# Opening of a two-layer transformer block: how c's rows reach the partitions, and which channels VectorE and TensorE sum

## Chip, cores and metric

The kernel runs on one core of a Trainium2 chip. The metric is device time in microseconds (us): the median of several executions. The kernel before takes 1632.78 us, the median of 3 runs (1631.76 to 1633.01).

## What is computed

The reference is a two-layer diffusion transformer with 256 latent tokens `x` and 256 context tokens `ctx`, 1024 features each. Each layer has a half feed-forward block, a mixer (attention, then mLSTM), and another half feed-forward block. Only the opening matters here: the modulation of the tokens by `c` (for latent tokens) and `c_ctx` (for context tokens), and the first product with the first feed-forward weights.

```
mod_lat = split(silu(c) @ ada_w[0] + ada_b[0], 9)       # 9 channels of 1024 numbers
mod_ctx = split(silu(c_ctx) @ ada_w[0] + ada_b[0], 9)
xm = h * (1.0 + scale) + shift                          # channels 0 (shift) and 1 (scale)
a, u = split(xm @ w_in, 2)
y = (silu(a) * u) @ w_out
```

So before the first token can be multiplied, two channels of `silu(c) @ ada_w` are wanted, for both vectors: 2 channels x 1024 features x 2 vectors, each a sum over 1024 numbers.

## The kernel before

**Tiles.** Features lie on the 128 partitions, in ND = 8 blocks `d` of 128; the 512 tokens (256 latent, then 256 context) lie along the free axis. Every f32 product is made of three F32R products: high part by high part, high by low, low by high. A value is split by a rounding copy on ScalarE (the high part) and a subtraction on VectorE (the low part).

**The opening, `start` (L1440 to L1599).** It loops over the eight feature blocks `d`. For each, a block of tokens (`in_xt`, 256 KB), a block of weights for the first four hidden tiles (`in_start_in`, 448 KB) and the block's two channels of `ada_w` (512 KB each) are loaded, all on SP's queue, in the order in which the code issues them. A channel is summed in one of two ways, by the table `PEDOT` (L48), which lists for each `d` the channels that go to TensorE:

- on TensorE (`by_pe`, L1488): 8 weight tiles of 128x128 from `in_ada_p`, each multiplied with two columns of silu(c) (`b.ct`), so 8 matmuls of 128x2 into the PSUM tile `dots`; ScalarE adds the bias (`moved`, L1498). Block 0 does both its channels in another form (`first_by_pe`, L1479: 8 matmuls of 2x256, a copy on ScalarE at L1483, two matmuls that turn the rows into columns, and a bias on VectorE at L1502);
- on VectorE (`by_dve`, L1504): for each vector one `scalar_tensor_tensor` of 128x1024 (L1510), which multiplies a row block of `ada_w` (`in_ada_w`) with `b.cb` and sums along the free axis. `b.cb` holds silu(c) and silu(c_ctx) repeated on all 128 partitions, 2 x 1024 numbers. A channel is two such dots; the bias follows at L1502.

`b.cb` is filled by two DMAs of 512 KB each (`silu_load`, L298 to L300: one row read 128 times), and ScalarE applies Silu to it in place (`silu`, L310).

When block `d`'s four numbers per feature are there, `modulated` (L1513) makes the modulated tokens by four ScalarE activations at L1525 (two of high parts, two in full), and `low` (L1530) subtracts to give the low parts: two 128x256 subtractions of tokens, one 128x896 subtraction of weights, on VectorE. ScalarE casts the weights at L1477, and also scales the raw tokens for later (L552). Then `products(d, i)` (L1546) gives 7 matmuls of 128x512 for each of i = 0 (high by high), 1 (high weights by low tokens) and 2 (low weights by high tokens), into seven PSUM tiles. The eighth output tile is made by `fill`, 3 matmuls per block, placed ahead of blocks 6 and 7 and at the end (`FILLED`, `EIGHTH`). After the opening the ordinary feed-forward units follow: their matmuls stand at L241, their casts at L225 and subtractions at L230, the gate at L579 and L580.

**What sets the order.** Nearly every instruction of `start` is pinned to program order on its engine (`pin`), so each engine runs them in the order of the code, each waiting for its own inputs. In the loop over `d` at L1565 that order is: load tokens and weights of block d+2, and channels of block d+3; cast the weights of block d+1; TensorE's dots for block d+1 (d of 2 and more); products(d, 0); low parts of block d's tokens; products(d, 1); for d below 2 TensorE's and VectorE's dots for block d+1; ScalarE's bias and the four activations for block d+1; low parts of the weights of d+1; for d of 1 and more VectorE's dots for block d+2; products(d, 2). DMAs use eight semaphores in turn, so an issue waits until the DMA eight places ahead of it has landed. Small work tiles `tmp` come from six buffers.

Of the kernel before, what the change touches and what calls it, by code (L numbers as in the profile page):

```python
# [11 lines left out]
BF16 = mybir.dt.bfloat16  # L12
# [9 lines left out]
T = 512  # L22
# [22 lines left out]

NSTART = 4

PEDOT = {0: (0, 1), 1: (1,), 2: (1,), 4: (1,), 6: (1,)}  # L48

WARM = 5  # L50

# [121 lines left out]
class Body:  # L173
# [23 lines left out]
    def mm(self):  # L197
        return self.t([P, 512], tag="mm", bufs=6, pool=self.pp)
# [218 lines left out]
    def pin(self, ins):  # L417

        return self.tc.keep_in_program_order(ins)
# [1020 lines left out]
def start(b):  # L1440
# [4 lines left out]
    nc, pin = b.nc, b.pin  # L1445
    V, S = nc.vector, nc.scalar
# [5 lines left out]
    ec = b.cols[:, BLOCK:].rearrange("p (d c v) -> p d c v", d=ND, c=2)  # L1452
    raws, blocks, ws, xs = {}, {}, {}, {}

    def load_dots(d):
        if d < ND:
            raws[d] = b.pair(F32)
            chs = PEDOT.get(d, ())
            for ch in range(2):
                if ch not in chs:  # L1460
                    dma(raws[d][ch], b.a["ada_w"][0, ch * ND + d])

            blocks[d] = []
            for i, ch in enumerate(chs):
                r, n = raws[d][ch], len(chs) * P
                dma(r, b.a["ada_p"][list(PEDOT).index(d), i])
                blocks[d] += [r[:, k * n : (k + 1) * n] for k in range(ND // len(chs))]

    def load(d):
        if d < ND:  # L1470
            dma(b.h[:, d, :], b.a["xt"][:, d, :])
            r = b.t([P, 1024], tag="raw", bufs=RAW)[:, : 7 * P]
            dma(r, b.a["start_in"][d][:, : 7 * P])
            ws[d] = [r] + b.pair(n=7 * P)

    def cast(d):
        pin(S.copy(ws[d][1], ws[d][0]))  # L1477
# [10 lines left out]
    def by_pe(d):  # L1488
        for i, ch in enumerate(PEDOT.get(d, ())):
            for k in range(ND):  # L1490
                mm(summed(d)[:, ch, :], blocks[d][k][:, i * P : (i + 1) * P], b.ct[:, k, :], start=k == 0, stop=k == ND - 1)

    def summed(d):
        return dots[:, TL + 4 * d : TL + 4 * d + 4].rearrange("p (c v) -> p c v", c=2)

    def moved(d):
        for ch in PEDOT.get(d, ()):
            pin(S.activation(ec[:, d, ch, :], summed(d)[:, ch, :], AF.Identity, bias=b.b01[:, d, ch : ch + 1]))  # L1498

    def biased(d, chs, x):  # L1500
        n = chs.stop - chs.start
        pin(V.tensor_tensor(out=ec[:, d, chs], in0=x[:, chs], in1=b.b01[:, d, chs, None].broadcast_to([P, n, 2]), op=ALU.add))  # L1502

    def by_dve(d):  # L1504
        chs = [ch for ch in range(2) if d < ND and ch not in PEDOT.get(d, ())]
        if chs:
            z = b.tmp().bitcast(BF16)
            for ch in chs:
                for v in range(2):
                    pin(V.scalar_tensor_tensor(z, raws[d][ch], 1.0, b.cb[:, v, :], ALU.mult, ALU.mult, accum_out=ec[:, d, ch, v : v + 1]))  # L1510
            biased(d, slice(chs[0], chs[-1] + 1), ec[:, d])

    def modulated(d):  # L1513
        jobs = []
# [14 lines left out]
    def low(l, x, h):  # L1529
        return pin(V.tensor_tensor(out=l, in0=x, in1=h.bitcast(F32), op=ALU.subtract))  # L1530
# [15 lines left out]
    def products(d, i):  # L1546
        w, x = ((1, 0), (1, 1), (2, 0))[i]
        for n, o in enumerate(acc):
            mm(o, ws[d][w][:, n * P : (n + 1) * P], b.x(d, BOTH)[x], start=not d and not i, stop=d == ND - 1 and i == 2)

    load_dots(0)
    load(0)
    b.silu_load(pin)
    load_dots(1)
    load(1)
    load_dots(2)
    b.setup_last()
    for _ in range(WARM):
        mm(dots[:, :TL], b.ones, b.ones[:, None, :].broadcast_to([P, 2, P]), start=True, stop=True)
    first_by_pe()  # L1560
    cast(0)
    modulated(0)
    low(ws[0][2], ws[0][0], ws[0][1])
    b.silu(pin)
    for d in range(ND):  # L1565
        n = d + 1
        load(d + 2)
        load_dots(d + 3)
        if d == EIGHTH[0]:
            load_eighth()  # L1570
        if n < ND:
            cast(n)
        if d == EIGHTH[1]:
            pin(S.copy(eighth[1], eighth[0]))
        if d > 1:
            by_pe(n)
        for k in FILLED.get(d, ()):
            fill(k)
        products(d, 0)
        for x in xs[d]:  # L1580
            last = low(*x)
        products(d, 1)
        if d < 2:
            by_pe(n)
            by_dve(n)
        moved(n)
        if n < ND:
            modulated(n)
            low(ws[n][2], ws[n][0], ws[n][1])
        if d:  # L1590
            by_dve(d + 2)
        if d == EIGHTH[1]:
            low(eighth[2], eighth[0], eighth[1])
        products(d, 2)
    fill(ND - 2)
    fill(ND - 1)
    b.fence[last.ins.engine] = last
# [63 lines left out]
def _layout(inputs):  # L1661
# [6 lines left out]
    part = lambda d, chs: w[:, :, list(chs), d].reshape(len(chs), -1, P, len(chs) * P).transpose(0, 2, 1, 3).reshape(-1, P, 1024)  # L1668
    A["ada_p"] = np.stack([np.resize(part(d, chs), (2, P, 1024)) for d, chs in PEDOT.items()])
    A["ada_w"] = f("ada_w").transpose(0, 2, 1).reshape(2, 72, P, D)  # L1670
# [78 lines left out]
```

## Time and profile before

| | us |
|---|---|
| median of 3 runs | 1632.78 (1631.76 to 1633.01) |
| the profiled execution, as timed | 1630.64 |
| its span in the profile | 1628.9 |
| start of the first product of tokens and weights | 10.63 |
| start of the first feed-forward unit after the opening (L241) | 66.01 |
| mean granted TensorE clock of the span | 0.998 |

The profiled execution took 1.74 us outside its span, and 2.14 us less than the median. In the profile, times run from the start of the span. A row of the timeline gives the start, the length, the engine, the line, the operation, the number of merged instructions, and in brackets the idle time before it with what ended it. SPq is the queue of SyncE, which issues the DMAs; PE is TensorE, DVE is VectorE, ACT is ScalarE.

### The profile page before, as it was taken

To read this page: it belongs to the slowest core of one execution; us is meant where nothing else is said; L and a number is where in the kernel's file an instruction comes from. 1 tells how busy PE (TensorE), PEld (TensorE's weight loads), DVE (VectorE), ACT (ScalarE), POOL (GpSimd) and SP (SyncE) were. 2 spreads that over 40 slices of the span, in tenths; PEclk is the share of its full clock that TensorE was granted. 3 is DMA by queue.
4 is the path that set the end of the run, shared out by engine and by line. 5 is a ranking of instruction groups with operands and counts; after the bars stand their busy time and mean duration, and the time that the engine had idled before them with its cause. 6 is when DMAs were issued, how large, how long until landed. Compare 5 with 4: busy or idle time off the path is not lost. (4 is left out here: it accounts for less than half of the span.)

```text
span 1628.9 us, 26573 instructions
## 1 busy us (share of the span) xinstructions
PE 1605.6 (99%) x10298; PEld 1449.8 (89%) x10298; DVE 1353.4 (83%) x2694; ACT 750.3 (46%) x1272; POOL 62.1 (4%) x76
## 2 busy tenths in 40 slices
PE   8999999999999999999999999999999999999998
PEld 6888888889988998889998998889999989999987
DVE  6799977749889879899986879789966968897687
ACT  5532223215676453316652444336652657566542
POOL 0000000001011100000000100000001000020000
PEclk9999999999999999999999999999999999999999
DMA  9677756422202447633345258713363342437552
GB/s 371 219 238 243 243 192 193 141 78 85 65 1 78 144 137 221 216 124 104 123 148 183 78 163 289 250 60 117 104 226 98 98 130 90 140 108 254 181 174 91
DMA packets 72494, 252.58 MB, mean 155 GB/s; under 512 B 7984, under 2 KB 10800, under 8 KB 72368
## 3 DMA queue, kind: packets, MB, share of 16 engines
q1 hardware_dynamic: 71792, 250.10, 47.3%
q8 instruction: 80, 1.31, 0.3%
q10 hardware_dynamic: 576, 0.79, 0.1%
q14 instruction: 46, 0.38, 0.1%
HBM read 249.81 MB, written 1.05 MB: 154 GB/s over the span
## 5 line engine op out<-in xcount | busy, mean ns | idle before, releaser
L241 PE MATMUL t<-t,t 128*128 128x256 f32 (+2 forms) x8412 | 1315.5, 317 | 7.3 <-ACT t L225 3.4
L241 PEld LDWEIGHTS t<-t,t 128*128 128x128 f32 x8412 | 1184.2, 188 | 126.4 <-ACT t L225 4.8
L225 ACT CAST t<-t 128x1024 fp32r<-128x1024 f32 (+3 forms) x521 | 428.5, 844 | 484.7 <-PE t L241 221.9
L230 DVE TENSOR_TENSOR t<-t,t 128x256 fp32r<-128x256 f32 (+2 forms) x740 | 514.0, 729 | 112.6 <-ACT t L225 108.9
L341 DVE SCALAR_TENSOR_TENSOR t<-t,t 128x1024 bf16<-128x1024 f32 x224 | 260.7, 1220 | 0.0
L579 ACT ACTIVATE t<-t 128x512 f32<-128x512 f32 (+1 forms) x71 | 34.3, 489 | 105.5 <-PE t L241 105.5
L932 PE MATMUL t<-t,t 128*128 128x256 f32 (+1 forms) x256 | 79.4, 310 | 0.0
L709 DVE SCALAR_TENSOR_TENSOR t<-t,t,t 128x256 f32<-128x256 f32 x96 | 42.7, 479 | 43.9 <-PE t L241 43.7
L933 PE MATMUL t<-t,t 128*128 128x256 f32 (+1 forms) x256 | 78.6, 307 | 0.1
L934 PE MATMUL t<-t,t 128*128 128x256 f32 (+1 forms) x256 | 78.5, 307 | 0.0
L580 DVE TENSOR_TENSOR t<-t,t 128x512 f32<-128x512 f32 (+1 forms) x71 | 38.9, 553 | 43.5 <-PE t L241 31.3
L475 POOL TENSOR_TENSOR t<-t,t 128x256 f32<-128x256 f32 x30 | 23.4, 780 | 1108.6 <-ACT t L465 1107.2
L1447 PE MATMUL t<-t,t 128*128 128x512 f32 (+2 forms) x276 | 57.3, 363 | 3.8 <-DVE t L1530 2.4
L860 PE MATMUL t<-t,t 128*128 128x512 f32 (+1 forms) x300 | 60.7, 364 | 0.0
L860 PEld LDWEIGHTS t<-t,t 128*128 128x128 f32 x300 | 51.4, 189 | 9.2 <-DVE t L854 0.4
L1447 PEld LDWEIGHTS t<-t,t 128*128 128x128 f32 (+1 forms) x276 | 45.8, 187 | 15.3 <-DVE t L1530 2.9
L465 ACT ACTIVATE t<-t 128x256 f32<-128x256 f32 x72 | 26.2, 413 | 65.7 <-DVE t L458 65.7
L933 PEld LDWEIGHTS t<-t,t 128*128 128x128 f32 x256 | 48.1, 188 | 3.3 <-DVE t L230 0.8
L932 PEld LDWEIGHTS t<-t,t 128*128 128x128 f32 x256 | 48.3, 189 | 2.7
L934 PEld LDWEIGHTS t<-t,t 128*128 128x128 f32 x256 | 48.1, 188 | 2.5
L532 ACT ACTIVATE t<-t,t 128x256 fp32r<-128x256 f32 x72 | 32.8, 503 | 30.1 <-DVE t L531 30.1
L632 DVE TENSOR_TENSOR t<-t,t 128x512 f32<-128x512 f32 x66 | 45.4, 687 | 0.4
(202 smaller groups left out, 1071.7 us busy)
## 6 DMA issues: line engine op xcount, KB each, us to landing
t<-in_ffn_in SPq DMA_DIRECT2D x168, 512.0 KB, 4.0
t<-in_ada_w SPq DMA_DIRECT2D x138, 512.0 KB, 4.2
t<-in_ffn_out SPq DMA_DIRECT2D x66, 512.0 KB, 4.5
t<-in_ffn_last SPq DMA_DIRECT2D x22, 512.0 KB, 3.6
t<-in_att_in SPq DMA_DIRECT2D x12, 512.0 KB, 3.6
t<-in_c SPq DMA_DIRECT2D x8, 512.0 KB, 7.6
t<-in_att_out SPq DMA_DIRECT2D x8, 512.0 KB, 3.6
t<-in_ml_qk SPq DMA_DIRECT2D x8, 512.0 KB, 3.7
```

The source lines that it names most:

```text
L225: self.behind(self.nc.scalar.copy(h, x))
L230: self.behind(self.nc.vector.tensor_tensor(out=ls, in0=xs, in1=hs.bitcast(F32), op=ALU.subtract))
L241: mm = lambda *k, **kw: self.nc.tensor.matmul(*k, skip_group_check=not group, **kw)
L341: ins = nc.vector.scalar_tensor_tensor(self.tmp().bitcast(BF16), r, 1.0, self.cb[:, v, :], ALU.mult, ALU.mult, accum_out=to)
L580: V.tensor_tensor(out=sl, in0=sl, in1=pu[:, :n], op=ALU.mult)
L632: add = lambda o, x, y: V.tensor_tensor(out=o, in0=x, in1=y, op=ALU.add)
L709: V.scalar_tensor_tensor(z, y[:, gg[0] - t0 : gg[1] - t0], gate()[:, v, d : d + 1], z, ALU.mult, ALU.add)
L860: pin(nc.tensor.matmul(o, gs[g], ws[k][w][:, i : i + n], start=k == k0 and g == w == 0, stop=k == k1 - 1 and g == 1,))
L932: mm(o, self.xh[:, k, c], wh, start=k == 0, stop=False)
L933: mm(o, self.xh[:, k, c], wl, start=False, stop=False)
L934: mm(o, self.xl[:, k, c], wh, start=False, stop=k == ND - 1)
L1447: mm = lambda *k, **kw: pin(nc.tensor.matmul(*k, **kw))
```

## The change

The core of the diff:

```diff
-PEDOT = {0: (0, 1), 1: (1,), 2: (1,), 4: (1,), 6: (1,)}
+PEDOT = {0: (0, 1), 1: (1,), 2: (1,), 3: (1,), 4: (1,)}
...
-    def by_dve(d):
+    def by_dve(d, *parts):
         chs = [ch for ch in range(2) if d < ND and ch not in PEDOT.get(d, ())]
-        if chs:
-            z = b.tmp().bitcast(BF16)
-            for ch in chs:
+        for i in parts:
+            if i < len(chs):
+                z, ch = b.tmp().bitcast(BF16), chs[i]
                 for v in range(2):
                     pin(V.scalar_tensor_tensor(z, raws[d][ch], 1.0, b.cb[:, v, :], ALU.mult, ALU.mult, accum_out=ec[:, d, ch, v : v + 1]))
-            biased(d, slice(chs[0], chs[-1] + 1), ec[:, d])
+                if i == len(chs) - 1:
+                    biased(d, slice(chs[0], chs[-1] + 1), ec[:, d])
...
+    rows = [(v, slice(i, i + T), b.tmp()) for v in range(2) for i in (0, T)]
+    for v, c, r in rows:
+        pin((V, nc.gpsimd)[v].memset(r, 0.0))
+    for v, c, r in rows:
+        pin(S.dma_start(r[::32, :], b.a["c2"][v : v + 1, c].broadcast_to([4, T])))
     load_dots(0)
     load(0)
-    b.silu_load(pin)
     load_dots(1)
...
     b.setup_last()
+    for v, c, r in rows:
+        pin(V.stream_shuffle(b.cb[:, v, c], r, [0] * 32))
+    b.silu(pin)
     for _ in range(WARM):
...
     low(ws[0][2], ws[0][0], ws[0][1])
-    b.silu(pin)
     for d in range(ND):
...
-        products(d, 1)
         if d < 2:
             by_pe(n)
-            by_dve(n)
+            by_dve(n, 0, 1)
+        else:
+            by_dve(n, 1)
         moved(n)
         if n < ND:
             modulated(n)
             low(ws[n][2], ws[n][0], ws[n][1])
-        if d:
-            by_dve(d + 2)
         if d == EIGHTH[1]:
             low(eighth[2], eighth[0], eighth[1])
-        products(d, 2)
+        if d:
+            by_dve(d + 2, 0)
+        for i in range(1, 3):
+            products(d, i)
```

It has three parts.

1. **c's rows.** The two DMAs of 512 KB on SP's queue are gone. Instead each row of 1024 is cut in two halves of 512; for each half a 128x512 tile is set to zero (two by VectorE, two by GpSimd), a DMA on ScalarE's queue puts the half row on partitions 0, 32, 64 and 96 (4 x 2 KB), and a VectorE `stream_shuffle` copies, within each group of 32 partitions, the first partition to all 32. Silu moves ahead of the copy of block 0's sums.
2. **Other channels on TensorE.** TensorE now sums channel 1 of blocks 1, 2, 3 and 4, where it was 1, 2, 4 and 6. VectorE sums both channels of blocks 5, 6 and 7, where it was 3, 5 and 7. Both engines make as many dots as before. For block 1 and 2 TensorE's dots also move ahead of products(d, 1).
3. **Halves.** Where VectorE sums both channels of a block, the two dots of channel 0 stand where all four stood, and the two of channel 1 come one loop pass later, behind the low parts of the next block's tokens.

Three places in the instruction order show it. First ScalarE, at its start. Before: Silu of the spread rows (tile t_77 is `b.cb`) stands behind the copy at L1483 and the activations of block 0.

```order
L319 ACTIVATE t_61<-t_61 128x16
L1483 COPY t_115<-t_88 2x256
L1477 CAST t_95<-t_93 128x896
L1525 ACTIVATE t_67<-t_66,t_61 128x256
L1525 ACTIVATE t_129<-t_66,t_61 128x256
L1525 ACTIVATE t_130<-t_66,t_61 128x256
L310 ACTIVATE t_77<-t_77 128x1024 x2
```

After: four DMA issues and Silu stand ahead of that copy. The waits are given in brackets; DMAHW1 is the DMA semaphore that the first `in_ada_p` transfer uses.

```order
L319 ACTIVATE t_61<-t_61 128x16 [waits DMAHW0_49]
L1556 DMA t_89<-in_c 4x512 [waits DVE_49]
L1556 DMA t_90<-in_c 4x512 [waits DVE_49]
L1556 DMA t_91<-in_c 4x512 [waits Pool_49]
L1556 DMA t_92<-in_c 4x512 [waits DMAHW1_49,Pool_49]
L310 ACTIVATE t_77<-t_77 128x1024 [waits DVE_49] x2
L1483 COPY t_131<-t_88 2x256 [waits PE_49]
```

So the copy of block 0's sums, on which the first product hangs, now runs behind Silu, and Silu behind the shuffles and the four small DMAs.

Second VectorE, around blocks 2 and 3. Before, between the low part of block 2's weights (the first row) and the low parts of block 2's tokens (t_68 is the tile of low parts of tokens) stand four dots of block 3:

```order
L1530 TENSOR_TENSOR t_141<-t_139,t_141 128x896
L1510 SCALAR_TENSOR_TENSOR t_233,t_61<-t_142,t_77 128x1024 x4
L1502 TENSOR_TENSOR t_61<-t_61 128x4
L1530 TENSOR_TENSOR t_68<-t_226,t_67 128x256
L1530 TENSOR_TENSOR t_68<-t_227,t_67 128x256
L1530 TENSOR_TENSOR t_192<-t_190,t_192 128x896
```

After, the same place holds two:

```order
L1531 TENSOR_TENSOR t_155<-t_153,t_155 128x896
L1510 SCALAR_TENSOR_TENSOR t_240,t_61<-t_156,t_77 128x1024 x2
L1502 TENSOR_TENSOR t_61<-t_61 128x2
L1531 TENSOR_TENSOR t_68<-t_233,t_67 128x256
L1531 TENSOR_TENSOR t_68<-t_234,t_67 128x256
L1531 TENSOR_TENSOR t_206<-t_204,t_206 128x896
```

Two dots of block 3 went to TensorE, where 8 matmuls of 128x2 now stand between products(1, 2) and products(2, 0); the 8 that stood ahead of products(5, 0) are gone.

Third VectorE, around blocks 5 and 6. Before: two dots of block 6, the low part of the eighth output tile's weights (128x1024), and then the low parts of block 5's tokens.

```order
L1530 TENSOR_TENSOR t_294<-t_292,t_294 128x896
L1510 SCALAR_TENSOR_TENSOR t_376,t_61<-t_295,t_77 128x1024 x2
L1502 TENSOR_TENSOR t_61<-t_61 128x2
L1530 TENSOR_TENSOR t_255<-t_253,t_255 128x1024
L1530 TENSOR_TENSOR t_68<-t_369,t_67 128x256
L1530 TENSOR_TENSOR t_68<-t_370,t_67 128x256
```

After: block 6 has four dots, two ahead of the low parts of block 5's tokens and two behind them.

```order
L1531 TENSOR_TENSOR t_315<-t_313,t_315 128x896
L1531 TENSOR_TENSOR t_267<-t_265,t_267 128x1024
L1510 SCALAR_TENSOR_TENSOR t_392,t_61<-t_316,t_77 128x1024 x2
L1531 TENSOR_TENSOR t_68<-t_384,t_67 128x256
L1531 TENSOR_TENSOR t_68<-t_385,t_67 128x256
L1510 SCALAR_TENSOR_TENSOR t_423,t_61<-t_316,t_77 128x1024 x2
L1502 TENSOR_TENSOR t_61<-t_61 128x4
```

Ahead of the tokens' low parts there are two dots in both; the two dots behind them are new. From the first four feed-forward units on, every engine's order is the same as before but for a few rows right behind the opening.

## Prediction

> **What bounds the kernel now.** I read the busy shares first, then TensorE's waits in the stretch that the change touches.
>
> ```profile
> span 1628.9 us, 26573 instructions
> PE 1605.6 (99%) x10298; PEld 1449.8 (89%) x10298; DVE 1353.4 (83%) x2694; ACT 750.3 (46%) x1272; POOL 62.1 (4%) x76
> ```
>
> TensorE is busy for 1605.6 of 1628.9 us. A gain can only come out of the 23.3 us in which it is not, or from a slow clock. TensorE's waits in the first 130 us:
>
> ```profile
> PE t L1447 <- DVE t L1530: 2.4, 1, 2.4
> PE t L1447 <- ACT t L1525: 0.9, 1, 0.9
> PE t L1447 <- DVE t L276: 0.9, 1, 0.9
> PE t L1447 <- ACT t L1483: 0.5, 1, 0.5
> ```
>
> One wait is large: 2.4 us for a low part by VectorE. TensorE's timeline has its place:
>
> ```profile
> 10.63 16.70 PE L1447 MATMUL t<-t,t 128*128 128x512 f32 x81 [0.95 <-ACT t L1525]
> 29.77 30.51 PE L1447 MATMUL t<-t,t 128*128 128x512 f32 x149 [2.43 <-DVE t L1530]
> 66.01 14.21 PE L241 MATMUL t<-t,t 128*128 128x512 f32 x62
> ```
>
> TensorE runs from 10.63 to 27.33, waits until 29.77, and then runs without a gap into the feed-forward units at 66.01. **Products of tokens and weights start at 10.63, and 2.43 us are lost once**; no other idle time is left between 10.63 and 130. Why VectorE is late is in its own timeline:
>
> ```profile
> 23.82 1.22 DVE L1510 SCALAR_TENSOR_TENSOR t<-t,t 128x1024 bf16<-128x1024 f32 x1
> ...
> 27.61 1.22 DVE L1510 SCALAR_TENSOR_TENSOR t<-t,t 128x1024 bf16<-128x1024 f32 x1
> ...
> 28.88 0.17 DVE L1502 TENSOR_TENSOR t<-t 128x4 f32<-128x4 f32 x1
> 28.96 1.76 DVE L1530 TENSOR_TENSOR t<-t,t 128x256 fp32r<-128x256 f32 x3
> ```
>
> The four dots of block 3 begin at 23.82 and hold the queue until the bias at 28.88: 1.265 us each. Only at 28.96 do the low parts of block 2's tokens start. ScalarE had made their inputs long before:
>
> ```profile
> 24.02 0.26 ACT L1498 ACTIVATE t<-t,t 128x2 f32<-128x2 f32 x1 [1.76 <-PE t L1447]
> 24.32 2.08 ACT L1525 ACTIVATE t<-t,t 128x256 fp32r<-128x256 f32 x4
> ```
>
> The four activations end at 26.40.
>
> **The change part by part.**
>
> *Other channels on TensorE.* Two of those four dots go: 2 x 1.265 = 2.53 us, so the low parts can start at 28.96 - 2.53 = 26.4, when their inputs are there too. TensorE comes there later than before, for 8 matmuls of 128x2 now stand in front:
>
> ```profile
> L1447 PE MATMUL t<-t,t 128*128 128x2 f32 x16 | 1.8, 246 | 0.0
> ```
>
> A set (16 passes) is 1.8 us. TensorE would want the low parts at 27.33 + 1.8 = 29.1, and they are there by about 27.2 (26.4 and two of 0.42). **The wait of 2.43 us goes.** The set is no added work: the one ahead of products(5, 0) is gone. On VectorE 20 dots remain 20.
>
> *What is late next.* Blocks 5 and 6 now lie back to back with four dots each. The durations there:
>
> ```profile
> L1510 DVE SCALAR_TENSOR_TENSOR t<-t,t 128x1024 bf16<-128x1024 f32 x20 | 24.5, 1223 | 2.0 <-ACT t L310 1.5
> L1530 DVE TENSOR_TENSOR t<-t,t 128x896 fp32r<-128x896 f32 x8 | 8.7, 1086 | 1.1 <-ACT t L1477 1.1
> L1530 DVE TENSOR_TENSOR t<-t,t 128x256 fp32r<-128x256 f32 x16 | 6.2, 421 | 1.0 <-ACT t L1525 0.8
> 44.37 2.90 DVE L1530 TENSOR_TENSOR t<-t,t 128x1024 fp32r<-128x1024 f32 x4
> ```
>
> I walk from the end of TensorE's dots for block 4 to the low parts of block 5's tokens. On ScalarE the bias and four activations, 2.4 us; on VectorE block 4's low tokens 0.8, two dots of block 5 and their bias 2.6, block 5's low weights 1.1, the eighth tile's (128x1024) 1.2, two dots of block 6 2.5, block 5's low tokens 0.8: 11.4. Neighbours overlap: the four subtractions at 44.37, one of each of these sizes and a second 128x256, last 2.90 for some 3.15, so 0.08 at each of six joints: 10.9. On TensorE products(3), products(4) and products(5, 0) are 49 matmuls, at 0.229 each (62 of that shape last 14.21 at 66.01): 11.2. TensorE comes 0.3 us after the low parts.
>
> Here the halves matter: with all four dots of block 6 in front, the low parts would come 2.5 us later and a wait of 2.2 would stand where now none is. Term: 0, at worst +0.4. The end of VectorE's opening moves closer to TensorE's; behind it stand idle times that take this up:
>
> ```profile
> 61.44 1.23 DVE L230 TENSOR_TENSOR t<-t,t 128x1024 fp32r<-128x1024 f32 x1 [1.51 <-ACT t L225]
> 63.92 1.22 DVE L230 TENSOR_TENSOR t<-t,t 128x1024 fp32r<-128x1024 f32 x1 [1.25 <-ACT t L225]
> 77.16 0.69 DVE L580 TENSOR_TENSOR t<-t,t 128x512 f32<-128x512 f32 x1 [3.15 <-PE t L241]
> ```
>
> *c's rows.* Removed: two transfers of 512 KB. SP's issues wait for landings eight places earlier, and so show them:
>
> ```profile
> 8.72 0.33 SPq L1448 DMA_DIRECT2D t<-in_ada_p  x1
> 10.96 0.33 SPq L327 DMA_DIRECT2D t<-in_vec  x1
> 12.24 0.33 SPq L328 DMA_DIRECT2D t<-in_const  x1
> 13.47 0.33 SPq L1448 DMA_DIRECT2D t<-in_xt  x1
> ```
>
> At 8.72 block 0's weights have landed, at 10.96 and 12.24 the two halves of c, at 13.47 block 1's first channel. Without c all later loads land 3.5 us earlier. That ends VectorE's early waits (1.49 us for Silu and 1.1 for a cast), but TensorE waited for none of them: 0 by itself.
>
> Added, on the path to the first product: the copy at L1483 now stands behind Silu.
>
> ```profile
> 2.61 0.22 ACT L319 ACTIVATE t<-t 128x16 f32<-128x16 f32 x1 [0.60 <-DMA t<-in_first]
> 8.67 0.36 ACT L1483 COPY t<-t 2x256 f32<-2x256 f32 x1 [5.84 <-PE t L1447]
> 11.47 1.99 ACT L310 ACTIVATE t<-t 128x1024 f32<-128x1024 f32 x2
> 2.59 0.43 SPq L1448 DMA_DIRECT2D t<-in_start_in  x1
> 6.17 0.33 SPq L1448 DMA_DIRECT2D t<-in_start_in  x1
> t<-in_first SPq DMA_DIRECT2D x1, 17.0 KB, 1.9
> L1399 POOL MEMSET t<- 64x512 f32 x1 | 0.5, 520 | 9.6 <-PE t L438 9.6
> L632 DVE TENSOR_TENSOR t<-t,t 128x512 f32<-128x512 f32 x66 | 45.4, 687 | 0.4
> ```
>
> No row shows VectorE's memset of 128x512 or a shuffle. Memset: between nothing and 0.69 (a 128x512 operation, L632); I take 0.52, GpSimd's 64x512, the nearest row. Shuffle: between nothing and, if it ran twice as long as L632, 1.4; I take 0.69. VectorE is free at 2.8 (its work at L323 waits for the same DMA as ScalarE's row at 2.61): memsets end at 3.3 and 3.8; GpSimd's are done by then. ScalarE issues at 0.43 each: 3.3, 3.8, 4.3; the fourth waits for the first `in_ada_p` transfer, which TensorE's dots at 5.01 had used: 4.8. A small DMA lands 1.9 after its issue: 5.2, 5.7, 6.2, 6.7. Shuffles run 5.2, 5.9, 6.6, 7.3 and end at 8.0. The second Silu takes 1.04: 9.05. The copy then starts at 9.05, not at 8.67: **+0.4 us** on the first product, and TensorE has nothing else to do there. Behind the shuffles VectorE has the bias at L1502, which needs that copy anyway; behind GpSimd's memsets nothing stands in the opening. On SP two issues take turns with the small DMAs on the eight semaphores: block 1's weights wait for the first of them (5.2; it was issued at 6.17), block 2's tokens for the fourth (6.7, before 13.47).
>
> Bounds of this term: nothing, if memsets and shuffles are short (Silu then ends before 8.67); +1.6, if each small DMA also waits for one 512 KB transfer (12.24 less 10.96, 1.28); +3.0, if they land behind all that SP had issued before them. The last of these, block 1's first channel, would land at 13.47 - 3.52 = 9.95; a shuffle and a Silu later it is 11.7. I take the first price, 0.4, since `in_first` is a DMA of this size.
>
> On this last choice a rule bears: by the Trainium skill, "DMA: Bandwidth & Descriptors", section "Queues, rings and completion order", each DMA engine goes round between the queues for which it has work, packet by packet. By it the small DMAs overtake what SP has queued, and the sum has the 0.4; with one line for all it would have the 3.0. No row here shows two loaded queues.
>
> *Sum.* -2.43 + 0.4 + 0 = **-2.0 us**. The profiled execution's 1630.64 becomes 1628.6. It lies 2.14 under the median of 1632.78, and I carry that along: the forecast for the median is 1632.78 - 2.0 = 1630.8.
>
> **The rivals.**
>
> *A second gain, the clock.* TensorE's granted clock, in four stretches:
>
> ```profile
> 7.89:11.30 3.41, 2.01 (x11) 1.20 (x10) 1.48 (x3) 2.52 (x5) 0.00 (x0) 1.00 1.01 334
> 11.30:14.71 3.41, 3.41 (x10) 2.63 (x9) 1.92 (x5) 2.77 (x5) 0.00 (x0) 0.50 1.03 415
> 28.37:31.78 3.41, 2.01 (x9) 1.67 (x10) 3.38 (x8) 2.70 (x7) 0.00 (x0) 1.00 1.03 397
> 31.78:35.20 3.42, 3.42 (x25) 3.13 (x24) 3.35 (x9) 1.07 (x2) 0.00 (x0) 1.00 1.09 409
> ```
>
> In columns: length, TensorE's busy time, then weight loads, VectorE, ScalarE, GpSimd, clock, DMA share, GB/s. After a stretch with 2.01 us busy of 3.41 the clock was 0.50 for 3.41 us, a loss of 1.7; after another with 2.01 it stayed at 1.00. The wait of 2.43 us lay across two stretches. If in other executions it falls into one, 1.0 busy of 3.41, the next may run at half speed, and the wait costs 2.43 + 1.7. The median's 2.14 over the profiled execution would fit that. Without the wait both go: 1630.8 - 1.7 = 1629.1, and less with a smaller start term. Against it: the offset may come from the opening's first stretch just as well, which stays. The Trainium skill, "TensorE: Matmul & The Clock Gate", section "What's actually happening", states such a rule: windows of 3413 ns that run freely and don't start with the kernel. By it the place of the wait in the window changes from run to run, and the trace's 3.41 us agrees.
>
> *c's rows come late, no gain.* The start term is 2.4 to 3.0, or TensorE meets VectorE again at blocks 5 and 6: the wait has only moved. -2.43 + 3.0 = +0.6: 1633.4. For it speaks that the DMA engines are 1.01 busy just then; against it the small size.
>
> *c's rows come late and the clock falls: slower.* If the fourth row lands only at 11.2, behind one more transfer, Silu ends at 11.2 + 0.69 + 1.04 = 12.95, and the first product starts 4.3 late, at 14.9. From a landing at about 9.1 (a start 2.4 late) the gain is gone. TensorE's sums of block 0 end at 8.6 (the copy takes them at 8.67); it would idle nearly all of 8.6 to 14.9, more than a whole stretch, and start at half clock for one stretch beyond the one that it has now, 1.7: -2.43 + 4.3 + 1.7 = +3.6, 1636.4.
>
> **How the numbers follow.** Forecast 0.53 (1629.7 to 1632.0), the clock's gain 0.25, late rows without gain 0.14, late rows with a cold clock 0.08. A measurement of this kernel can tell about 0.2%, 3.3 us, from no change; that bounds the signs: faster is below 1629.5, slower above 1636.0. So faster has the clock rival's 0.25, same the forecast and the late rows, 0.67, slower 0.08. The range reaches from 1628.2, the clock rival with a start term of nothing (1628.7) and 0.5 of the early waits, to 1633.6, late rows; outside lie the last rival and a part of the clock's, under 0.2.
>
> **What would show it.** Right: the first product at about 11.0, no TensorE wait over 0.4 between there and 130, L241 at about 64.0, VectorE's four shuffles done by 8.0. Wrong: the copy at L1483 starting after 10 (late rows); a wait at L1447 for L1531 near 45 or 52 (VectorE at blocks 5 and 6); L241 before 63 or a clock below 1.00 at another place (the clock). It would be wrong altogether if the feed-forward units behind the opening, whose order I take as unchanged, began to wait.

## The result, and the profile after

The changed kernel takes 1636.71 us (median of 10 runs, 1633.98 to 1640.27); the kernel before, beside it, 1632.62 (10 runs, 1630.25 to 1633.01). The ratio is **1.0028, with a 95% interval of 1.0018 to 1.0038: 4.6 us slower** (0.0028 x 1632), 2.9 to 6.2; the two medians lie 4.1 apart. The forecast was 1630.8, the range ended at 1633.6. The profiled execution of the changed kernel was the shortest of its ten, 1633.98 with a span of 1632.2.

TensorE's timeline, in the columns of before:

```profile
5.17 3.61 PE L1447 MATMUL t<-t,t 128*2 128x256 f32 x16
12.95 1.01 PE L1447 MATMUL t<-t,t 2*128 2x2 f32 x4 [4.17 <-ACT t L1483]
14.92 52.80 PE L1447 MATMUL t<-t,t 128*128 128x512 f32 x256 [0.96 <-ACT t L1526]
67.56 62.72 PE L241 MATMUL t<-t,t 128*128 128x512 f32 x276
```

The wait of 2.43 us at block 2 is gone: from 14.92 on, 256 matmuls run in one piece to 67.56. But they start at 14.92 where they started at 10.63, because the turning matmuls waited 4.17 us for the copy at L1483. ScalarE's timeline shows why the copy is late:

```profile
3.15 2.79 ACTq L1556 DMA_DIRECT2D t<-in_c  x4
10.32 1.06 ACT L310 ACTIVATE t<-t 128x1024 f32<-128x1024 f32 x1 [7.69 <-DVE t L1564]
11.59 1.06 ACT L310 ACTIVATE t<-t 128x1024 f32<-128x1024 f32 x1 [0.21 <-DVE t L1564]
12.55 0.34 ACT L1483 COPY t<-t 2x256 f32<-2x256 f32 x1
```

It issues the four small DMAs from 3.15 and otherwise has nothing to run for 7.69 us, until the first two shuffles are done; Silu runs, and the copy, whose input was ready at 8.78, starts at 12.55 instead of 8.67. VectorE's timeline, one step further back:

```profile
2.63 1.03 DVE L1554 MEMSET t<- 128x512 f32 x2
7.59 0.01 DVE L1564 LOAD_MASK_SELECT t<-t  x1 [3.93 <-DMA t<-in_c]
7.62 0.73 DVE L1564 STREAM_SHUFFLE t<-t 128x512 f32<-128x512 f32 x1
9.55 0.01 DVE L1564 LOAD_MASK_SELECT t<-t  x1 [1.20 <-DMA t<-in_c]
9.57 0.72 DVE L1564 STREAM_SHUFFLE t<-t 128x512 f32<-128x512 f32 x1
...
10.83 0.73 DVE L1564 STREAM_SHUFFLE t<-t 128x512 f32<-128x512 f32 x1
```

The first half row landed at about 7.6, the second at about 9.55; the last two shuffles waited for nothing but the one before. Memsets (0.52 each) and shuffles (0.73, one every 0.63) cost what the prediction took. **The landings are what is late.** The clock, last, by stretches (busy times of TensorE, its weight loads, VectorE, ScalarE, GpSimd, then the granted clock, the DMA share, GB/s):

```profile
8.19:11.61 3.42, 0.59 (x3) 0.08 (x1) 2.16 (x7) 1.08 (x2) 0.00 (x0) 1.00 1.01 382
11.61:15.02 3.41, 1.11 (x5) 1.03 (x5) 0.91 (x3) 2.88 (x5) 0.00 (x0) 0.50 1.02 410
15.02:18.43 3.41, 3.41 (x10) 2.73 (x10) 3.38 (x6) 2.27 (x5) 0.00 (x0) 0.50 1.05 412
18.43:21.85 3.42, 3.42 (x23) 3.11 (x23) 1.50 (x4) 1.69 (x4) 0.00 (x0) 1.00 1.04 419
462.16:465.58 3.42, 3.42 (x13) 2.87 (x12) 3.30 (x8) 1.57 (x5) 1.56 (x1) 0.50 0.00 0
```

Each of the two stretches at half clock follows one in which TensorE was nearly idle (0.59 and 1.11 us busy); before, there was one, 11.30 to 14.71. A further one at 462.16 stands where the kernel before has none in its profile. It comes and goes in kernels that do the same there: the profiles of six of the twelve variants below have it, between 457.8 and 462.5, and of six they don't. So I take it for a matter of the execution and don't put it down to the change; one profile of each kernel can't show that.

In this pair of profiles the loss can be added up. The start is 4.3 later, the wait of 2.4 is gone, and 0.3 is made up behind it: L241 comes 1.55 later (67.56 for 66.01). Both kernels run products at half clock for about 3.4 us (before from 11.30 to 14.71, changed from 14.92 to 18.43). The stretch that the changed opening has more lies over TensorE's wait and costs only 0.4, in the turning matmuls (1.01 for 0.60), which is a part of the 4.3. The stretch at 462.16, with TensorE busy throughout, costs half its length, 1.7. Together that is about the 3.3 by which the spans differ (1632.2 and 1628.9).

Since these stretches come and go, one profile is a thin base for what they cost on average. The rows show a granted clock of 1.00 or 0.50 and nothing between. Each timed run lists its mean granted clock; the mean over the runs that are compared says how much half-clock time it has on average: (1 - clock) x 2 x 1632 us. For the kernel before it is 0.9975 (the 29 runs beside e1 to e4), 8 us; for the changed kernel 0.9947, 17 us. Of the extra 9 us half is lost, if TensorE has work all the while: up to 4.6 us, the size of the whole loss; less where a stretch lies over a wait, as above. Three executions of the kernels timed below took 1998 to 2200 us at a mean clock of 0.68 to 0.75; medians, ratios and clocks are without them.

### The profile page after: what moved, and what is told of

Same layout as the page of the kernel before. It is cut to its first block, busy times and chain, and to the rows that moved or that the text cites. A ratio compares the mean times of both kernels' runs of the same rounds, so it can differ in the third digit from the quotient of the medians.

```text
span 1632.2 us, 26584 instructions
## 1 busy us (share of the span) xinstructions
PE 1607.3 (98%) x10298; PEld 1452.5 (89%) x10298; DVE 1356.8 (83%) x2704; ACT 749.7 (46%) x1272; POOL 63.2 (4%) x78
## 5 line engine op out<-in xcount | busy, mean ns | idle before, releaser
L241 PE MATMUL t<-t,t 128*128 128x256 f32 (+2 forms) x8412 | 1317.5, 318 | 7.2 <-ACT t L225 3.3
L241 PEld LDWEIGHTS t<-t,t 128*128 128x128 f32 x8412 | 1186.1, 188 | 126.3 <-ACT t L225 4.6
```

Of the source, the lines that this page charges most:

```text
L241: mm = lambda *k, **kw: self.nc.tensor.matmul(*k, skip_group_check=not group, **kw)
```

## The experiments

Twelve kernels. "Before" is each one's own comparison on its chip; us against before is (ratio - 1) x 1632. Start is the first product of tokens and weights, L241 the first feed-forward unit, half the time at half clock in the opening, all three in the profiled execution; clock is the mean over the timed runs.

| kernel | median | ratio (95%) | us against before | start | L241 | half | clock |
|---|---|---|---|---|---|---|---|
| before | 1632.62 | | | 10.63 | 66.01 | 3.4 | 0.9975 |
| changed | 1636.71 | 1.0028 (1.0018 to 1.0038) | +4.6 | 14.92 | 67.56 | 6.8 | 0.9947 |
| e1 channels, halves, order | 1633.94 | 1.0004 (0.9995 to 1.0012) | +0.7 | 10.94 | 67.42 | 10.2 | 0.9955 |
| e2 rows alone | 1638.89 | 1.0037 (1.0025 to 1.0049) | +6.0 | 15.37 | 71.48 | 6.8 | 0.9962 |
| e3 changed, Silu back | 1631.94 | 0.9996 (0.9987 to 1.0004) | -0.7 | 11.77 | 65.00 | 3.4 | 0.9963 |
| e4 changed, nine fillers | 1632.05 | 1.0006 (0.9998 to 1.0015) | +1.0 | 15.15 | 66.19 | 0 | 0.9974 |
| e5 = e1, dots back | 1629.09 | 0.9982 (0.9973 to 0.9990) | -2.9 | 10.48 | 63.13 | 3.4 | 0.9975 |
| e6 = e5, three fillers | 1627.94 | 0.9973 (0.9962 to 0.9983) | -4.4 | 11.18 | 62.87 | 0 | 0.9983 |
| e7 before, three fillers | 1631.19 | 0.9996 (0.9987 to 1.0005) | -0.7 | 10.85 | 65.43 | 0 | 0.9984 |
| e8 changed, dots back | 1634.57 | 1.0015 (1.0006 to 1.0024) | +2.4 | 15.28 | 68.80 | 6.8 | 0.9959 |
| e9 = e8, rows early | 1632.37 | 0.9998 (0.9989 to 1.0006) | -0.3 | 14.18 | 67.11 | 6.8 | 0.9969 |
| e10 = e9, three fillers | 1631.51 | 0.9995 (0.9986 to 1.0003) | -0.8 | 13.23 | 65.55 | 3.4 | 0.9975 |
| e11 = e5, no halves | 1630.55 | 0.9987 (0.9978 to 0.9996) | -2.1 | 11.46 | 64.62 | 0 | 0.9981 |
| e12 = e1, three fillers | 1632.88 | 1.0007 (0.9998 to 1.0016) | +1.1 | 10.68 | 63.72 | 0 | 0.9969 |

**Theory 1, after the result:** the rows come late, hold up the copy, and let the clock fall; channels and halves gain what was predicted. **The rivals:** the moved channels and halves cost the time (theory 2), or half-clock stretches at random places do (theory 3).

### e1 and e2: each part alone

e1 is the changed kernel with c loaded as before:

```diff
-    rows = [(v, slice(i, i + T), b.tmp()) for v in range(2) for i in (0, T)]
...
     load(0)
+    b.silu_load(pin)
...
-        pin(V.stream_shuffle(b.cb[:, v, c], r, [0] * 32))
-    b.silu(pin)
...
     low(ws[0][2], ws[0][0], ws[0][1])
+    b.silu(pin)
```

> The changed channels, the halves and the new order alone; c's rows as before (two 512 KB transfers, Silu behind block 0's work). Theory 1 (the small DMAs land late, Silu holds up the copy at L1483, the idle TensorE falls to half clock; channels and halves gain): the first product back at 10.6, no wait of 2.4 at block 2, no new wait at blocks 5 and 6, L241 at about 63.6 (66.0 - 2.4), median about 1630.2, that is 2.4 under the kernel before. Theory 2 (the moved channels and halves cost the time, through a VectorE that is now tighter; late rows are mostly hidden): a wait of 1 to 3 us at blocks 3 to 6, L241 not before 67, median 1 to 3 us above the kernel before.

e2 is the kernel before with the rows part alone, the same lines the other way round.

> c's rows by small DMAs and shuffles alone; channels, halves and order as before. Theory 1: the copy at L1483 ends near 12.9 and the first product of the steady stream starts at about 14.9, 4.3 later than before, with one more half-clock stretch of 3.4 us; a wait for VectorE at block 2 of 2.4 less what VectorE makes up by earlier loads (about 1 to 2.4) stays; L241 at 70 to 72, median 4.5 to 6.5 above the kernel before. Theory 2: at most 1 us above it.

The rows alone cost 6.0 us (4.1 to 8.0), as theory 1 expected, with the start at 15.37. TensorE's timeline of e2 keeps the wait at block 2 whole:

```profile
15.37 17.48 PE L1447 MATMUL t<-t,t 128*128 128x512 f32 x81 [0.96 <-ACT t L1525]
35.23 36.41 PE L1447 MATMUL t<-t,t 128*128 128x512 f32 x175 [2.39 <-DVE t L1530]
71.48 58.87 PE L241 MATMUL t<-t,t 128*128 128x512 f32 x259
```

But e1, which had to bring 2.4, brings nothing (+0.7, -0.8 to +2.0). **Both theories missed here**: there is no wait by VectorE at blocks 3 to 6 either. TensorE's timeline and its clock in e1:

```profile
10.94 2.54 PE L1447 MATMUL t<-t,t 128*128 128x512 f32 x7 [0.95 <-ACT t L1526]
14.38 10.83 PE L1447 MATMUL t<-t,t 128*128 128x2 f32 x41 [0.90 <-DMA t<-in_ada_p]
```

```profile
8.51:11.92 3.41, 2.01 (x10) 1.37 (x9) 1.80 (x4) 2.84 (x6) 0.00 (x0) 1.00 1.00 357
11.92:15.34 3.42, 2.52 (x9) 1.64 (x8) 2.47 (x5) 2.45 (x4) 0.00 (x0) 0.50 1.03 415
15.34:18.75 3.41, 3.41 (x15) 3.28 (x15) 1.70 (x4) 1.66 (x3) 0.00 (x0) 0.50 1.04 408
18.75:22.16 3.41, 3.41 (x9) 2.64 (x8) 2.16 (x5) 3.13 (x7) 0.00 (x0) 0.50 1.04 423
```

Three stretches at half clock, not one. Behind the seven matmuls of products(0, 0) stand TensorE's dots of block 1, which the change moved ahead of products(0, 1). They wait 0.90 us for their weights, and at half clock they take twice as long: in e1 16 passes last 3.6 us, a whole stretch.

```profile
L1447 PE MATMUL t<-t,t 128*128 128x2 f32 x16 | 3.6, 354 | 0.9 <-DMA t<-in_ada_p 0.9
```

In 15.34 to 18.75 TensorE is busy all the time, but until 17.8 with matmuls of 2 columns, and the next stretch is at half clock again. That gave theory A for the next runs: these dots are little work for the clock, and where they stand decides.

### e5, e8, e12: where TensorE's dots of blocks 1 and 2 stand

e5 is e1, and e8 the changed kernel, with these dots back where they stood before the change:

```diff
         if d < 2:
+            products(d, 1)
             by_pe(n)
             by_dve(n, 0, 1)
...
-        for i in range(1, 3):
+        for i in range(1 if d > 1 else 2, 3):
             products(d, i)
```

> The changed channels and halves alone (c's rows as before), and TensorE's dots of blocks 1 and 2 put back behind products(d, 1), where they stood before the change. Theory A (these dots of 128x2 count as little work for the clock; ahead of products(0, 1) they make or prolong a half-clock stretch): no wait for the second in_ada_p transfer, one half-clock stretch of 3.4 us in the opening, not three; L241 at about 63.6, a mean clock of the runs of about 0.9975 as in the kernel before (0.9955 in the run with the changed channels alone), median 2 to 2.4 under the kernel before. Theory B (the clock falls for another reason, or the loss lies in the moved channels themselves): mean clock 0.9955 again and a median 0 to 2 above the kernel before, as with the dots ahead.

> The changed kernel with TensorE's dots of blocks 1 and 2 put back behind products(d, 1); c's rows late as they are. Theory A: the first product still at about 14.9 behind an idle 4.2, so at least one half-clock stretch stays, but mean clock 0.996 where the changed kernel has 0.9947, and a median 1 to 2.5 under the changed kernel's (about 1634.5 to 1635.5). If the late start alone makes the half-clock stretches: 1636 to 1637 as the changed kernel.

e5 is 2.9 us faster than before (1.6 to 4.4), with one half-clock stretch and L241 at 63.13:

```profile
10.48 52.82 PE L1447 MATMUL t<-t,t 128*128 128x512 f32 x256 [0.95 <-ACT t L1526]
63.13 67.03 PE L241 MATMUL t<-t,t 128*128 128x512 f32 x295
```

Theory A holds in e5: against e1 the ratio falls by 0.0022 (3.6 us, give or take 1.9) and the clock returns from 0.9955 to 0.9975. In e8 the same edit brings 2.1 us against the changed kernel; as a difference of two ratios, each uncertain by 0.0010 and 0.0009, that alone is hardly above its error, but the clocks are apart (0.9947 and 0.9959, 0.0007 and 0.0003 uncertain), 3.9 us of half-clock time. The profiles don't show this gain: L241 comes at 68.80 in e8 and at 67.56 in the changed kernel, since e8 started 0.4 later and its second half-clock stretch reached to 20.63 and not 18.43. So in the changed kernel the cost of the dots' place rests on averages and is not shown by its rows.

Is it the half-clock stretch ahead that makes the dots costly, or their place by itself? e12 is e1 with three filler matmuls (128x256, on constants; the first product overwrites their result), which fill TensorE's two short waits in the start:

```diff
         pin(S.copy(row, o))
+        filler(1)
         for ch in range(2):
             mm(summed(0)[:, ch, :], row[:, ch * P : (ch + 1) * P], b.two, start=True, stop=True)
+        filler(2)
```

> The changed channels, halves and order alone (c's rows as before, TensorE's dots of blocks 1 and 2 ahead of products(d, 1) as in the changed kernel) with the three filler matmuls; it differs from the earlier run with fillers only by the place of these dots. Theory A1 (the dots ahead cost only because a half-clock stretch comes first: at half clock they fill a whole stretch by themselves): no half-clock stretch in the opening, mean clock of the runs 0.9985 or more, median 1628 to 1629, as with the dots put back. Theory A2 (16 passes of 2 columns beside the 0.9 us wait for the second in_ada_p transfer are too little work for the clock even when it is full): one or more half-clock stretches between 13 and 22, mean clock 0.997 or less, median 1630 to 1632.

Neither as put. The profiled execution has no half-clock stretch in the opening, as A1 expected, but a wait of 1.76 us:

```profile
10.68 1.88 PE L1447 MATMUL t<-t,t 128*128 128x512 f32 x7
14.32 49.57 PE L1447 MATMUL t<-t,t 128*128 128x2 f32 x249 [1.76 <-DMA t<-in_ada_p]
```

The median, 1632.88, and the clock, 0.9969, are A2's. Against e6, the same with the dots back, the place costs 5.5 us here (0.0034). The waits (1.76 for 0.28) explain 1.5 of it and the clocks (0.9969 for 0.9983) 2.3, together 3.8; the 5.5 is uncertain by 2.2. With c's 1 MB on SP's queue block 1's in_ada_p (which the expectation calls the second) lands at 14.3, and dots that want it at 12.6 must wait. So the early place has two prices: this wait, where c is loaded as before, and the clock. In the changed kernel, where that load is no longer behind the 1 MB, TensorE has no such wait, so only the second can be left.

### e4, e6, e7: filler matmuls against the half clock

e4 is the changed kernel with nine fillers where TensorE waits for the copy (the first place of the diff above, nine instead of one).

> The changed kernel with nine more matmuls of 128x256 on TensorE (on constants, into a PSUM tile that the first product overwrites) behind the sums of block 0, so that TensorE works while it waits for the copy at L1483; the copy is as late as in the changed kernel. Theory 1 and theory 3: the first product at 14.9 still, but at clock 1.00 where the changed kernel has a second stretch of 0.50, L241 at about 65.8 (67.56 - 1.75), median 1.7 to 2.7 under the changed kernel. If the half-clock stretch costs nothing, because the products of the opening wait for other engines anyway: the same L241 and median as the changed kernel's.

e4 starts as late as the changed kernel, and L241 comes 1.4 us earlier:

```profile
9.47 4.18 PE L1447 MATMUL t<-t 128*128 128x256 f32 x18
13.59 0.60 PE L1447 MATMUL t<-t,t 2*128 2x2 f32 x4
15.15 51.21 PE L1447 MATMUL t<-t,t 128*128 128x512 f32 x256 [0.96 <-ACT t L1528]
66.19 64.08 PE L241 MATMUL t<-t,t 128*128 128x512 f32 x282
```

The ratio is 0.0022 under the changed kernel's: 3.6 us, give or take 2.2, more than the one stretch that the profile of the changed kernel lets expect. The clocks fit (0.9974 for 0.9947, 8.8 us at half speed): other executions of the changed kernel must have more such stretches than the one that was profiled, its shortest. Work that computes nothing, in a wait, wins back most of the loss. That shows the clock's part.

> The run before this one in the list (changed channels and halves, c's rows as before, dots of blocks 1 and 2 put back) and three filler matmuls of 128x256 on constants: one while TensorE waits for the copy at L1483, two while it waits for block 0's activations. Theory A: no half-clock stretch in the opening at all, the first product at 10.6 to 11.0, L241 at about 62 (51.1 us of products behind it), median 3.5 to 4.1 under the kernel before, that is at about 1628. If the first half-clock stretch costs nothing: the same as without the fillers.

> The kernel before with the same three filler matmuls and nothing else. Theory A: the half-clock stretch of the opening is gone (1.7 us), the wait of 2.4 at block 2 stays, L241 at about 64.3, median 1.7 under the kernel before. If it moves the half-clock stretch to the wait of 2.4 instead: no gain.

e6 is e5 and e7 the kernel before with the three fillers. TensorE's timeline of e6:

```profile
11.18 6.99 PE L1447 MATMUL t<-t,t 128*128 128x512 f32 x37
18.45 44.58 PE L1447 MATMUL t<-t,t 128*128 128x512 f32 x219 [0.28 <-ACT t L1532]
62.87 67.48 PE L241 MATMUL t<-t,t 128*128 128x512 f32 x297
```

e6 is the fastest of all, 1627.94, by ratio 4.4 us under before (2.8 to 6.2): one wait of 0.28 behind the first product, no half clock in the opening, L241 at 62.87. It starts 0.7 later than e5 and gains 1.5 by ratio (0.0009, which is not above the errors of the two). In e7 the stretch goes as expected (clock 0.9984), but the gain is 0.7 and within its error (-2.1 to +0.8, which still holds the expected 1.7): L241 moves from 66.01 to 65.43 only. The start is 0.2 later, a wait of 0.32 us for ScalarE's activations is new, and the 2.38 for VectorE stays:

```profile
18.24 8.53 PE L1447 MATMUL t<-t,t 128*128 128x512 f32 x44 [0.32 <-ACT t L1531]
29.15 36.44 PE L1447 MATMUL t<-t,t 128*128 128x512 f32 x175 [2.38 <-DVE t L1536]
```

Where another engine is close behind, as here, a faster TensorE waits.

### e3, e9, e10: the rows

e3 is the changed kernel with the shuffles and Silu behind block 0's activations:

```diff
-    for v, c, r in rows:
-        pin(V.stream_shuffle(b.cb[:, v, c], r, [0] * 32))
-    b.silu(pin)
...
     low(ws[0][2], ws[0][0], ws[0][1])
+    for v, c, r in rows:
+        pin(V.stream_shuffle(b.cb[:, v, c], r, [0] * 32))
+    b.silu(pin)
```

> The changed kernel with its four shuffles and Silu moved behind block 0's four activations and weights' low part, so that the copy at L1483 no longer stands behind them; the small DMAs are as in the changed kernel. Theory 1: the copy back at about 8.7, the first product at about 10.6, L241 at 63.3 to 63.6, no second half-clock stretch at 14 to 18, median 2.4 under the kernel before and 4 to 6.5 under the changed one. Theory 2: the first product early, but the time is lost again at blocks 3 to 6, so the median is within 1 us of the changed kernel's. Theory 3 (most of the time is lost by half-clock stretches that come at random places): the median stays 2 or more above the kernel before although the opening ends early.

```profile
11.77 3.57 PE L1447 MATMUL t<-t,t 128*128 128x512 f32 x23 [0.95 <-ACT t L1526]
15.80 49.36 PE L1447 MATMUL t<-t,t 128*128 128x512 f32 x233 [0.46 <-DVE t L1531]
65.00 65.22 PE L241 MATMUL t<-t,t 128*128 128x512 f32 x287
```

The copy no longer waits for Silu, and 5.2 us of the ratio are won back (0.9996 for 1.0028). Its rows show why it isn't 2.4 under before: the block 0 dots ended at 9.76 here (8.63 in the kernel before, but 9.45 in e11 too, which loads c as before), so the start is 11.77; and the shuffles, now ahead of block 0's low tokens, make a wait of 0.46. Behind the stretch with that wait one at half clock follows (clock of the runs 0.9963). Block 1's dots, which e3 leaves ahead of products(0, 1), stand in the same stretch; e3 can't tell the two apart.

Why do the small DMAs land so late? The first was issued at 3.15. Ahead of it, SP had issued in_first, two in_ada_p, in_xt, in_start_in and (at 3.05) an in_ada_w: 17 + 1024 + 256 + 448 + 512 KB, 2.31 MB. What SP's queue (q1) had moved when the first packet of the first small DMA started, at 6.53, and of the second, issued at 4.29, at 8.31 (packets, MB, share; q10 is ScalarE's queue, with the first DMA's packets; windows 0 to 6.53 and 0 to 8.31):

```profile
q1 hardware_dynamic: 602, 1.43, 67.7%
```

```profile
q1 hardware_dynamic: 802, 2.12, 74.3%
q10 hardware_dynamic: 9, 0.01, 0.3%
```

So 1.43 and 2.12 MB had gone first, of 1.79 (without the in_ada_w) and 2.31 queued, 80 and 92%. The 8 KB on a queue of their own overtook little here; they came when most of what had been issued ahead of them elsewhere had gone (theory Q of the next expectation). e9 puts that to the test: e8 with the memsets and the small DMAs as the first work of their engines, in the order first halves, second halves.

```diff
     b.setup()
+    b.rows = [(v, slice(i, i + T), b.tmp()) for i in (0, T) for v in range(2)]
+    for v, c, r in b.rows:
+        b.pin((nc.vector, nc.gpsimd)[v].memset(r, 0.0))
+    for v, c, r in b.rows:
+        b.pin(nc.scalar.dma_start(r[::32, :], b.a["c2"][v : v + 1, c].broadcast_to([4, T])))
     b.setup_rest()
```

> The changed kernel with TensorE's dots of blocks 1 and 2 put back behind products(d, 1) and with the memsets and small DMAs of c's rows as the first work of their engines (the DMAs issued from about 1.3 to 3.2, ahead of ScalarE's table load, instead of 3.15 to 5.9); the rows are taken in the order first halves, second halves. Theory Q (in the changed kernel the small DMAs waited behind the transfers that SP had queued before them): they land by about 5.5, the shuffles are done by about 7, Silu by about 8.5, the copy at L1483 is again set by TensorE (8.6 to 9.1), first product at 10.6 to 11.0, one half-clock stretch, L241 at 63 to 64, median 2.5 to 3.5 under the kernel before. Theory S (such a DMA takes its 4.4 us from issue to landing by itself): rows by 7.5, Silu at about 9.4, first product at about 11.4, median 2 under the kernel before. If the shuffles or Silu's place are the cost and not the landing: first product at 13 or later and a median 2 or more above the kernel before.

> The run before this one in the list with the three filler matmuls (one behind the sums of block 0, two behind the matmuls that turn them). Theory Q with the clock: no half-clock stretch in the opening, L241 at about 62, median at 1628 or a little under, 3.5 to 4.5 under the kernel before. If early loads bring something beside the start: under 1627.5.

VectorE's and ScalarE's timelines of e9:

```profile
6.35 0.73 DVE L1560 STREAM_SHUFFLE t<-t 128x512 f32<-128x512 f32 x1
8.51 0.01 DVE L1560 LOAD_MASK_SELECT t<-t  x1 [1.43 <-DMA t<-in_c]
```

```profile
1.54 2.73 ACTq L1616 DMA_DIRECT2D t<-in_c  x4
11.83 0.34 ACT L1483 COPY t<-t 2x256 f32<-2x256 f32 x1
```

Issued at 1.54, the first half row still lands only at 6.3. My number for theory Q (5.5 for all) is missed, theory S's 4.4 us is nearer for the first and misses the second (8.5, issued at 2.68: 5.8). By the bytes Q holds in part: the first packet started at 5.37, when SP's queue had moved 1.03 MB:

```profile
q1 hardware_dynamic: 412, 1.03, 56.6%
```

in_first and the two in_ada_p, issued at 1.17 and at 1.64, are 1.07; but the second in_ada_p was issued a tenth of a microsecond behind the small DMA, not ahead of it. The second small DMA started at 6.37, with 1.34 MB gone of the 1.79 issued before it:

```profile
q1 hardware_dynamic: 566, 1.34, 63.5%
```

So there is no strict line: that one overtook a quarter. The start is 14.18, a microsecond earlier than in e8 for an issue 1.6 earlier, since SP starts its transfers at once; by ratio e9 gains 2.8 on e8 (0.0017, give or take 2.0), and e9 and e10 only reach the kernel before (-0.3 and -0.8, both within error). e10 was to reach 1628 and misses it because TensorE still waits 1.41 us for the copy and one half-clock stretch stays. A small DMA with no transfer beside it was not tried, and no row shows when a small DMA's packets were ready to go. So a long latency of its own, or packets that are made late, is not excluded; that in e9 the second took a microsecond longer than the first, behind more bytes, speaks for the queue.

### e11: are the halves worth anything?

```diff
-        else:
-            by_dve(n, 1)
...
-            by_dve(d + 2, 0)
+            by_dve(d + 2, 0, 1)
```

> The changed channels with c's rows as before and TensorE's dots put back (median 1629.1 in its run), but without the halves: all four of VectorE's dots of a block stand together, where the first half stands. By the prediction's walk a wait for the low parts of block 5's tokens of 2.2 us appears between 40 and 55, L241 at about 65.3, median 2 to 2.5 above the run with halves, about 1631.3. If the halves do nothing: no such wait, 1629.1.

```profile
46.31 18.47 PE L1447 MATMUL t<-t,t 128*128 128x512 f32 x80 [1.58 <-DVE t L1531]
64.62 65.67 PE L241 MATMUL t<-t,t 128*128 128x512 f32 x289
```

The wait appears, at 44.7 and 1.58 long (2.2 expected). By ratio the halves are worth 0.8 us (0.0005, not above its error), by the wait 1.6.

## Where the prediction was wrong, and where right

- **The wait at block 2 goes, -2.43: right.** It stands in none of the kernels with the changed channels, and it stays, 2.4, in e2 and e7, which keep the old ones. e5, which has neither the new rows nor the moved dots, measures -2.9 (-4.4 to -1.6), halves included.
- **Blocks 5 and 6, a term of 0: right.** The changed kernel has no wait there, and without halves e11 has 1.58 for the predicted 2.2.
- **c's rows, +0.4: the step that failed.** The step was "A small DMA lands 1.9 after its issue", taken from in_first. They landed 4.4 and 5.3 after it (7.6 from 3.15, about 9.55 from 4.29), so the copy started at 12.55 and not at 9.05, and the start moved by 4.3. in_first had been issued at 0.73, with no transfer queued; the small DMAs had about 2 MB before them. A row from an empty machine was used for a busy one. That this is the step is shown by e2 (the rows alone lose 6.0) and e3 (with the copy no longer behind Silu 5.2 come back); why they land so late is open, as said under e9. The upper bound, +3.0, failed too: it had one shuffle and one Silu behind a last landing at 9.95, but from the landing at 9.55 on three shuffles ran in a line to 11.56, and at half clock the turning matmuls took 1.01 and not 0.60. The rule that I weighed, that an engine goes round between queues packet by packet ("DMA: Bandwidth & Descriptors" of the Trainium skill, section "Queues, rings and completion order"), would have the 8 KB overtake. Here they did so only in small part: 1.43 of 1.79 and 2.12 of 2.31 MB went first. Whether that goes against the rule or the packets came to their queue late, no row tells.
- **The price of the rows is 5.4 us**, more than the 4.3 by which the start moved: e8 against e5 (0.0033, give or take 0.0012), 6.0 in e2. L241 of e8 is 5.7 later than e5's: the start is 4.8 later, and the rest is the longer half clock.
- **TensorE's dots moved ahead of products(d, 1): a step I costed at nothing.** The text says "The set is no added work", which counts TensorE's time but not its clock. In the order with c loaded as before it costs 3.6 (e1 against e5), the wait of 0.90 included. In the changed kernel it costs about 2.1 us by ratio (e8), hardly above the error, and no row of the profile shows it.
- **Sum:** -2.9 (e5) + 5.4 (rows, e8 against e5) + 2.1 (dots, changed against e8) = +4.6. It closes by construction and shows nothing by itself, the three being steps from before to e5, to e8 and to the changed kernel; e2, on another path, gives 6.0 for the rows.
- **The rivals.** *Late rows and a cold clock: slower* had the start (14.9) and one more stretch at half clock right and gave 1636.4. That both are so near is partly luck: it reached 14.9 by a landing at 11.2 and one shuffle, where the rows have 9.55 and three; its 1.7 for the stretch was 0.4 in the profile; and its sum has 6.0 for the rows and none for the dots. *The clock's second gain* went the other way: the wait at block 2 wasn't followed by a half-clock stretch in any profile here that has it, and the change brought more of them.

"First product at about 11.0" and "VectorE's four shuffles done by 8.0" were the signs that failed first (14.92 and 11.56); "no TensorE wait over 0.4 up to 130" held from 14.92 on.

## What to carry to other kernels

A DMA's latency is to be taken from a row with the same transfers queued ahead of it, on whichever queue: replacing 1 MB by 32 KB gained nothing at the place where the 32 KB still came behind about 2 MB, and it turned a load off the path into one on it, because Silu was moved ahead of the copy. Before moving matmuls, look at which clock stretch they fall into: in e1 matmuls of two columns and waits bunched together kept the clock at half for three stretches. Filler matmuls in a wait can bring it back (nine in e4, three in e6 and e7); three did not suffice in e10, where a half-clock stretch stays in the opening, nor in e12, where the mean clock is 0.9969. When one edit is three, time them one by one: here one part gains 2.9 and two others lose 7.5 (of which the 2.1 for the dots is uncertain), and the part that gains, with fillers, is 4.4 us faster than before.

## What the runs showed of the hardware that was not expected

- Small DMAs on ScalarE's queue started when SP's queue had moved 1.43 and 2.12 MB of the 1.79 and 2.31 MB issued ahead of them; in e9 the second started at 1.34 of 1.79.
- A stretch of 3.41 us with TensorE busy throughout, most of its 15 passes 128x2, was followed by one at 0.50 (e1). A stretch with 2.46 busy of 3.42 (e4, 13.25 to 16.67) was not, one with 2.95 of 3.41 (e3, 13.70 to 17.11, dots of 128x2 in it) was. Busy time alone does not tell what the clock counts; by what measure it counts stays open.

```profile
13.25:16.67 3.42, 2.46 (x13) 1.78 (x13) 2.34 (x6) 2.89 (x7) 0.00 (x0) 1.00 1.02 380
16.67:20.08 3.41, 3.41 (x25) 3.10 (x24) 3.34 (x6) 1.92 (x5) 0.00 (x0) 1.00 1.02 399
```

```profile
13.70:17.11 3.41, 2.95 (x21) 2.67 (x21) 3.31 (x10) 3.02 (x4) 0.00 (x0) 1.00 1.04 405
17.11:20.53 3.42, 3.42 (x10) 2.64 (x9) 2.69 (x5) 2.11 (x6) 0.00 (x0) 0.50 1.02 415
```

- A `stream_shuffle` of 128x512 f32 takes 0.73 us and comes with a mask load of 0.01 each time; a memset of that size on VectorE takes 0.52.
